# Loading the head of each partition in four strided DMAs instead of one

## The chip, the cores and the metric

The kernel runs on one core of a Trainium2 chip. Such a core has engines that work beside each other and meet only at semaphores: VectorE (DVE) and ScalarE (ACT) copy data inside the on-chip memory, SyncE (SP) issues transfers, and 16 DMA engines move the data between the main memory (HBM) and the on-chip memory, which has 128 partitions. TensorE (PE) and GpSimd (POOL) have no data to work on here. The metric is the device time of one execution in microseconds; three runs of the kernel before gave a median of 197.13 us (197.04 to 197.38).

## The reference

The kernel enlarges images by a factor of two, each pixel becoming a square of four:

```python
batch, channels, h, w = 16, 64, 64, 64          # float32
for i in range(2 * h):
    for j in range(2 * w):
        result[:, :, i, j] = x[:, :, i // 2, j // 2]
```

No arithmetic is done. 16.78 MB are read and 67.11 MB written, 83.89 MB in all.

## The kernel before

The input is taken as 65536 image rows of 64 numbers (256 bytes). Partition p holds 512 rows in a run, so its share of the input is a contiguous 128 KB and its share of the output a contiguous 512 KB (`xp` and `op`, lines 173 to 176). A single tile `mem` holds everything: the whole input of a partition at its far end (`xt`, line 188), and ahead of it room for the enlarged rows.

**Loads.** Lines 192 to 195 issue three loads on SP: rows 0 to 31 of every partition (the head, 8 KB per partition, `HEAD = 32`), rows 32 to 287 (64 KB) and rows 288 to 511 (56 KB). Each covers all 128 partitions, so each is 128 descriptors, 8 for each DMA engine. `begin_before_barrier` (lines 13 to 33) takes the first `EARLY = 3` instructions of SP, which are these loads, and moves them ahead of the barrier at which all engines meet at the start, so that SP issues them before anything else.

**Copies and stores.** The loop of lines 204 to 216 goes over nine groups of rows (`rows`, line 181: 54, 38, 54, 61, ... 62). For each group VectorE copies the first part of the rows enlarged into the room (line 213), ScalarE the rest (line 214), and SP stores the group (line 215). In the first group VectorE has 53 rows and ScalarE one; in the others the shares are about 5 to 3. Groups lie alternately at the start of the room and at its far end, where they overwrite input rows that have been used, so a copy waits for the store two groups before.

**Order of the work.** A framework puts in the semaphores: a copy waits for the loads that brought its rows, a store for the copies of its group. There are eight semaphores for DMAs, used in turn. All transfers are issued by SP and stand in one queue on each DMA engine in the order of issue. `close_early` (lines 80 to 151) arranges the end of the program: all semaphores are cleared early, but for the last store's, on which SP waits at the very end.

Of the kernel before, what the change touches and what calls it, by code (L numbers as in the profile page):

```python
# [6 lines left out]

EARLY = 3  # L10


def begin_before_barrier(nc):
# [5 lines left out]
    sp = mybir.EngineType.SP  # L19
    loads = [i for i in body.instructions if i.engine == sp][:EARLY]  # L20
    for load in loads:
# [132 lines left out]
@with_exitstack  # L154
def kernel(
    ctx: ExitStack,
    tc: tile.TileContext,
    x: bass.AP,
    scale_factor: int,
    out: bass.AP,  # L160
):
    nc = tc.nc
    nc.at_finalize(begin_before_barrier)
    nc.at_finalize(close_early)
    P = nc.NUM_PARTITIONS
    s = int(scale_factor)
    B, C, H, W = x.shape
    R = B * C * H // P
    fdt = x.dtype

    xp = x.rearrange("b c h w -> (b c h) w").rearrange("(p r) w -> p r w", p=P)
    op = out.rearrange("b c (h hd) w -> (b c h) (hd w)", hd=s).rearrange(
        "(p r) w -> p r w", p=P
    )

    rows = [54, 38, 54, 61, 54, 63, 63, 63, 62]
    GROW = s * s
    FREE = 79
    WF = FREE * GROW * W
    assert sum(rows) == R
    mem_pool = ctx.enter_context(tc.tile_pool(name="mem", bufs=1))
    mem = mem_pool.tile([P, WF + R * W], fdt, name="mem")
    xt = mem[:, WF:].rearrange("p (r w) -> p r w", r=R)

    HEAD = 32
    cuts = [0, HEAD, R // 2 + HEAD, R]
    for lo, hi in zip(cuts, cuts[1:]):
        nc.sync.dma_start(out=xt[:, lo:hi], in_=xp[:, lo:hi])  # L195

    def expanded(r0, r1):
        return (
            xt[:, r0:r1].unsqueeze(2).unsqueeze(4).to_broadcast([P, r1 - r0, s, W, s])
        )  # L200

    r0 = 0
    before = (0, 0)
    for n, k in enumerate(rows):
        size = k * GROW * W
        at = 0 if n % 2 == 0 else WF + r0 * W - size
        assert at >= before[1] or at + size <= before[0]
        before = (at, at + size)
        u = mem[:, at : at + size].rearrange(
            "p (k a w b) -> p k a w b", k=k, a=s, w=W  # L210
        )
        kv = k - 1 if n == 0 else k * 5 // 8 & ~1
        nc.vector.tensor_copy(out=u[:, :kv], in_=expanded(r0, r0 + kv))  # L213
        nc.scalar.copy(out=u[:, kv:], in_=expanded(r0 + kv, r0 + k))  # L214
        nc.sync.dma_start(out=op[:, r0 : r0 + k, :], in_=u)  # L215
        r0 += k
# [35 lines left out]
```

## Time and profile before

| what | time or share |
|---|---|
| median of three runs | 197.13 us (197.04 to 197.38) |
| the profiled execution | 196.92 us |
| its span, first to last instruction | 195.6 us |
| VectorE busy | 52.3 us, 27% |
| ScalarE busy | 42.1 us, 21% |
| DMA packets, share of 16 engines' span | 99.2% (1728 packets, 83.89 MB) |
| mean rate over the span | 429 GB/s |
| the three loads, from issue to landing | 4.7, 23.6 and 40.1 us |
| first copy on VectorE, 128x13568 | 14.3 us, from 24.11 us on |

The profile is of one execution on the chip. A row of work names the source line, the engine, the operation and the tiles, with its time; idle time is put down to what ended it. "SPq" is SP's queue of instructions: the transfers that it issues, not their data. The DMA share adds up the packets that the DMA engines moved, as a share of 16 engines' time.

### The profile page before, as it was taken

The page shows a single profiled execution, that of the slowest core. Times are in us where ns is not written, and L with a number is a line of the kernel's source. Part 1 is how long each engine was busy: PE and PEld are TensorE (multiplying, and loading weights), DVE is VectorE, ACT ScalarE, POOL GpSimd, SP SyncE. Part 2 cuts the span into 40 slices and gives each one's busy share as a digit, 9 for nine tenths or more (in the row PEclk, how much of TensorE's full clock was granted, in tenths as well). Part 3 has the DMA queues.
Part 4 walks back from the last instruction along what each step waited for, and adds up shares of the span by engine and source line. Part 5 has one row for each costly group of instructions (what it writes and reads, how often), then busy time and mean ns, then how long its engine had stood idle before and what let it go on. Part 6 is the DMA issues. An engine that isn't in the chain of part 4 may idle for free.

```text
span 195.6 us, 102 instructions
## 1 busy us (share of the span) xinstructions
DVE 52.3 (27%) x9; ACT 42.1 (21%) x10; POOL 0.2 (0%) x4
## 2 busy tenths in 40 slices
DVE  0000099940026091053008204500540073000000
ACT  2000000160029700059500004970000073000000
POOL 0000000000000000000000000000000000000000
DMA  9999989889899989999999899999999999999994
GB/s 429 429 429 429 402 375 563 375 362 543 362 436 390 555 362 418 486 409 409 409 420 532 362 531 433 422 422 422 422 422 422 422 422 422 422 435 545 467 428 208
DMA packets 1728, 83.89 MB, mean 429 GB/s; under 512 B 192, under 2 KB 192, under 8 KB 192
## 3 DMA queue, kind: packets, MB, share of 16 engines
q1 hardware_dynamic: 1728, 83.89, 99.2%
HBM read 16.78 MB, written 67.11 MB: 429 GB/s over the span
## 4 chain that ended last, share of the span: by engine, by line
DMA 65%; ACT 11%; DVE 7%; SPq 0%; issue 0%; DVEq 0%; ACTq 0%
DMA out_dram<-mem 53%; DMA mem<-in_x_dram 12%; ACT mem L214 11%; DVE mem L213 7%; SPq L195 0%; DVEq L213 0%; ACTq L214 0%; SPq L215 0%
## 5 line engine op out<-in xcount | busy, mean ns | idle before, releaser
L213 DVE COPY mem<-mem 128x9728 f32<-128x9728 f32 (+3 forms) x9 | 52.3, 5818 | 110.9 <-DMA out_dram<-mem 86.8
L214 ACT COPY mem<-mem 128x6400 f32<-128x6400 f32 (+5 forms) x9 | 40.8, 4530 | 119.4 <-DMA out_dram<-mem 84.2
L214 ACT ACT_TABLE_LOAD x1 | 1.3, 1283 | 1.7 <-PEq L233 1.7
L233 POOL MEMSET const-bfloat16-1.0<- 128x1 bf16 x1 | 0.1, 102 | 0.0
L233 POOL MEMSET const-uint8-127<- 128x1 uint8 x1 | 0.1, 102 | 0.0
L233 POOL MEMSET const-float32-1.0<- 128x1 f32 x1 | 0.1, 99 | 0.0
L233 POOL MEMSET const-float32-0.0<- 128x1 f32 x1 | 0.1, 98 | 0.2 <-issue 0.2
## 6 DMA issues: line engine op xcount, KB each, us to landing
out_dram<-mem SPq DMA_DIRECT2D x3, 8064.0 KB, 32.4
out_dram<-mem SPq DMA_DIRECT2D x3, 6912.0 KB, 22.9
out_dram<-mem SPq DMA_DIRECT2D x1, 7936.0 KB, 32.3
out_dram<-mem SPq DMA_DIRECT2D x1, 7808.0 KB, 29.3
mem<-in_x_dram SPq DMA_DIRECT2D x1, 7168.0 KB, 40.1
out_dram<-mem SPq DMA_DIRECT2D x1, 4864.0 KB, 26.7
mem<-in_x_dram SPq DMA_DIRECT2D x1, 1024.0 KB, 4.7
mem<-in_x_dram SPq DMA_DIRECT2D x1, 23.6
```

The lines of the kernel that those rows point to most:

```text
L213: nc.vector.tensor_copy(out=u[:, :kv], in_=expanded(r0, r0 + kv))
L214: nc.scalar.copy(out=u[:, kv:], in_=expanded(r0 + kv, r0 + k))
L233: nc = _bacc.Bacc("TRN2", target_bir_lowering=False, num_devices=1)
```

## The change

The head becomes 48 rows (12 KB per partition) instead of 32, and it is loaded by four DMAs instead of one. The first covers partitions 0, 8, 16, ... (16 of them), the second 4, 12, 20, ... (16), the third 2, 6, 10, ... (32) and the fourth all odd ones (64). Each partition's head is still one contiguous piece. The second load then begins at row 48 instead of 32 and still ends at row 287; the third is as before. There are six loads instead of three, and `EARLY` is 6 so that all of them stay ahead of the barrier.

```diff
-EARLY = 3
+EARLY = 6
...
-    HEAD = 32
-    cuts = [0, HEAD, R // 2 + HEAD, R]
+    HEAD = 48
+    for first, step in ((0, 8), (4, 8), (2, 4), (1, 2)):
+        some = slice(first, P, step)
+        nc.sync.dma_start(out=xt[some, :HEAD], in_=xp[some, :HEAD])
+    cuts = [HEAD, R // 2 + 32, R]
     for lo, hi in zip(cuts, cuts[1:]):
         nc.sync.dma_start(out=xt[:, lo:hi], in_=xp[:, lo:hi])
```

## The prediction

> **What bounds the kernel now.** I read the busy table first, then the DMA queue, the chain that ended last, the waits, and short windows over the start. From the page, parts 1, 3 and 4:
>
> ```profile
> span 195.6 us, 102 instructions
> DVE 52.3 (27%) x9; ACT 42.1 (21%) x10; POOL 0.2 (0%) x4
> ...
> q1 hardware_dynamic: 1728, 83.89, 99.2%
> ...
> DMA out_dram<-mem 53%; DMA mem<-in_x_dram 12%; ACT mem L214 11%; DVE mem L213 7%; SPq L195 0%; DVEq L213 0%; ACTq L214 0%; SPq L215 0%
> ```
>
> VectorE and ScalarE work for a quarter of the span; the 16 DMA engines are busy for 99.2% of it. The chain does name copies (11% and 7%), but it is a chain of releases, and those copies run beside transfers queued earlier. The trace's records of single DMA packets settle this: laid end to start they form 16 strings, each of 5.24 MB with no gap over 20 ns, from a first packet at 1.00 to 1.48 us to a last end at 194.78 to 195.21 us; the last write is reported at 195.56 us. So the time is three pieces: about 1.0 us to the first packet, about 194 us of busy engines, 0.35 us to the last report. Only what starts the engines later or earlier, slows a packet, or opens a gap can move it.
>
> The timeline, DMA issues (last column: us to landing) and windows (last two columns: DMA share and GB/s; a packet counts in one window only, so single values swing):
>
> ```profile
> 0.00 1.32 SPq L195 DMA_DIRECT2D mem<-in_x_dram  x3
> 1.72 1.28 ACT L214 ACT_TABLE_LOAD   x1 [1.72 <-PEq L233]
> 24.03 0.41 ACT L214 COPY mem<-mem 128x256 f32<-128x256 f32 x1 [21.03 <-DMA mem<-in_x_dram]
> 24.11 17.29 DVE L213 COPY mem<-mem 128x13568 f32<-128x13568 f32 x2 [24.11 <-DMA mem<-in_x_dram]
> ...
> mem<-in_x_dram SPq DMA_DIRECT2D x1, 1024.0 KB, 4.7
> ...
> 0.00:1.00 1.00, 0.00 (x0) 0.00 (x0) 0.20 (x4) 1.00 0.00 0
> 1.00:1.50 0.50, 0.00 (x0) 0.00 (x0) 0.00 (x0) 1.00 1.26 262
> 1.50:2.00 0.50, 0.00 (x0) 0.28 (x1) 0.00 (x0) 1.00 0.67 213
> 2.00:2.50 0.50, 0.00 (x0) 0.50 (x1) 0.00 (x0) 1.00 1.07 442
> ```
>
> The reader is to see three things. Nothing moves for 1.0 us after the first issue. For another microsecond the rate is about half of the later 429 GB/s. And the first copy starts at 24.11 us, when the second load is in: the 1024 KB head, landed at 4.7 us, is used by nobody alone.
>
> **The change part by part.** The sum is made against the profiled execution: 196.92 us, of which 195.6 are the span, and 0.2 below the median of 197.13.
>
> Bytes and packets: an engine had 8 packets of 8192 B (309 ns when running) and 8 of 65536 B (2418 ns) for the first two loads. It gets 8 of 12288 B and 8 of 61440 B. By the slope between those rows, (2418-309)/57344 = 0.0368 ns per byte, they take 460 and 2267 ns; 8 x (309 + 2418) and 8 x (460 + 2267) ns are 21.8 us both. No change. Three DMAs more are three more 4-byte completion packets per engine, 9 ns each: +0.03.
>
> Issues: three more instructions on SP. The three of before start at 0, 0.42 and 0.89 us, so about 0.45 us each, and SP reaches the barrier at 2.8 instead of 1.4 us. Nobody behind that barrier has work before 24 us except the table load. The queue stays fed: descriptors of the n-th small DMA can start at about 1.0 + 0.45 n us, and one packet of 460 ns per engine covers each step. Were an engine to outrun it, that costs some 0.05 us.
>
> Start: the 16 engines' first packets start between 1003 and 1482 ns (mean 1194), one engine after another while the 128 descriptors are laid out. With 16 descriptors I expect them within about 60 ns. But the engines that began first paid most in their first packets (the head cost 0.1 to 0.65 us more than 8 x 309 ns; mean 0.42), and none ended its first packet before 1558 ns. So the gain is what the two last engines have over the others at the end: 195.21 and 195.15 against about 195.0. I take -0.2; bounds 0 and -0.5 (start spread and a third of the ramp gone).
>
> Rate of the small DMAs: before has no DMA over less than 128 partitions, so the cost is bounded. From below: full rate, 0. From above: each of the eight 12288-byte packets of an engine at twice its duration, 8 x 0.46 = +3.7. The nearest row for "one packet on each of 16 engines, all at once" is the set of first packets, which took 325 to 856 ns, mean 630, twice the 309 of the running ones. I take a doubling for DMA 0 and DMA 1, which are just that (one packet per engine), and steady packets for the other two, which have two and four per engine: 2 x 0.46 = +0.92.
>
> [...]
>
> Waits: the first copy on VectorE waits for five loads instead of two, and the two parts of ScalarE and the first store on SP get the same added waits. All but the last are long done. A wait instruction takes 17 to 50 ns, so VectorE starts up to 0.1 us later behind the landing, and with it the first store (issued at 38.48 us) by up to 0.2 us. What hides this: the engines still work on the third load until 40.04 to 40.61 us, and an issue takes 1.0 to 1.48 us to its first packet, so 39.5 to 39.96. The cover is 0.1 to 0.6 us. If it is gone, the excess, at most 0.1 us, is a gap. I take 0.
>
> The instruction order of the changed kernel puts ScalarE's added waits ahead of its table load. So 1.28 us move from 1.7 us to behind the second load, at 24 us, ahead of the one-row copy of 0.41 us: done by 25.8 us. Only the first store waits for that copy, and VectorE's 14.3 us until 38.4 us cover it by over 12 us; without that cover it would cost 1.3 us. The copies, the nine stores, and the size and order of the third load stay.
>
> Sum: -0.20 + 0.92 + 0.03 = +0.75 us. Span 196.35, that execution 197.7, and on the median's footing 197.9 us.
>
> **The rivals.**
>
> *No DMA is slowed (other side).* The four small DMAs run at full rate and only the start shrinks: -0.17, 196.96 us, at best -0.5, 196.6 us. For it: no packet after the first two of an engine is slow anywhere in the trace, whatever its size, and the second load's packets at its start took 2418 to 2422 ns. Against it: every one of those was part of a 128-partition transfer, in which each engine has its own eight partitions. It decides for faster if the two 16-partition DMAs lose less than the 0.2 us that the start gives. To pass 0.2% (0.39 us, about what a measurement of this kernel can tell from no change) the first packets' excess must shrink too, not only the spread.
>
> *The whole head is slowed.* If neighbouring engines also hinder each other in the 32- and 64-partition DMAs, all eight small packets double: 3.7, less what the start spread lets the engines slip past each other (0.2 to 0.5) and less the 0.2 at the start: about +3.1, 200.2 us. For it: the engines' packets follow in step, 309 ns each, so two that meet once meet again. Against it: these two DMAs together cover 96 partitions, evenly. [...]
>
> *The queue runs dry.* If DMAs 1 to 3 arrive just after the engines are through with the one before, each pays the ramp of 0.42 us again: 3 x 0.42 = +1.26, less 0.2: 198.2 us. For it: 0.45 us per issue against 0.46 us per packet is a tie. Against it: the ramp of the first DMA puts the engines 0.3 us behind the queue.
>
> *The change does not do what it says?* It does start with a smaller DMA, but nobody uses the head earlier: the first copy reads 53 rows and the head has 48, so it still ends its wait with the load of rows 48 to 287. No gain can come from earlier copies.
>
> **How the numbers follow.** Two slowed DMAs 0.33 (own range 197.5 to 198.5); no DMA slowed 0.32, of which 0.10 are faster by over 0.2% and 0.22 within it; whole head 0.27; dry queue 0.08. Slower by over 0.2%: 0.33 + 0.27 + 0.08, less 0.02 for small losses, which go to faster for a ramp that shrinks more than I think: 0.66, within 0.22, faster 0.12. The range goes from 196.7 (leaving out the best starts, about 0.08) to 200.3 (leaving out the upper part of the whole-head case, about 0.1).
>
> **What would show it.** In the profile after: 12288-byte packets of about 460 ns (rival 1) or 900 ns (in DMA 0 and 1 alone, or in all four); first packets within 60 ns of each other; the landing of the load of rows 48 to 287, now 24.0 us, at 24.8 (forecast), 23.8 (rival 1) or 27.1 us (whole head), and the first copy right behind it, with everything later shifted by the same. A gap between the third load and the first store would mean that the added waits matter. I would be wrong if no small packet is slowed, or if the 32- and 64-partition DMAs are slowed too.

## The result and the profile after

The changed kernel takes 199.92 us (median of 4 runs, 199.56 to 200.45) where the kernel before took 197.19 us beside it (197.04 to 197.38): a ratio of 1.014, interval 1.0116 to 1.0165. It is slower by 2.7 us. The forecast was slower, at 197.9 us, in a range of 196.7 to 200.3.

The page of the changed kernel (the profiled execution took 199.96 us), parts 1, 3 and 6; the last column of part 6 is microseconds from issue to landing:

```profile
span 198.6 us, 109 instructions
DVE 52.3 (26%) x9; ACT 42.0 (21%) x10; POOL 0.2 (0%) x4
...
q1 hardware_dynamic: 1776, 83.89, 98.5%
...
mem<-in_x_dram SPq DMA_DIRECT2D x1, 7680.0 KB, 24.5
...
mem<-in_x_dram SPq DMA_DIRECT2D x1, 768.0 KB, 7.0
```

The copies cost what they did. The span is 3.0 us longer, the bytes are the same, and the share of busy DMA engines fell from 99.2 to 98.5%: 0.8% of 195.6 us was 1.6 us not busy, 1.5% of 198.6 us is 3.0, averaged over the 16, so half of the loss is idle engines and the rest slower packets. The largest of the small DMAs, 768 KB over 64 partitions, took 7.0 us to land. At the 429 GB/s of the span before it is 1.8 us of work.

The timeline of the changed kernel over the first 60 us:

```profile
0.00 2.49 SPq L195 DMA_DIRECT2D mem<-in_x_dram  x4
...
2.53 1.06 SPq L198 DMA_DIRECT2D mem<-in_x_dram  x2
27.09 1.28 ACT L217 ACT_TABLE_LOAD   x1 [27.09 <-DMA mem<-in_x_dram]
27.12 17.29 DVE L216 COPY mem<-mem 128x13568 f32<-128x13568 f32 x2 [27.12 <-DMA mem<-in_x_dram]
28.38 0.40 ACT L217 COPY mem<-mem 128x256 f32<-128x256 f32 x1
41.48 3.98 SPq L218 DMA_DIRECT2D out_dram<-mem  x2
```

The first copy starts at 27.12 instead of 24.11 us, right behind the load of rows 48 to 287. All 3.0 us are lost by then, and everything later is shifted by the same: the first store is issued at 41.48 instead of 38.48 us. The table load did move behind that load (1.28 us from 27.09 us on), and VectorE's copy, which ends at 41.41 us, covers it.

The windows of the changed kernel (last two columns: DMA share and GB/s) show where the time goes:

```profile
1.00:1.50 0.50, 0.00 (x0) 0.00 (x0) 0.00 (x0) 1.00 0.85 246
1.50:2.00 0.50, 0.00 (x0) 0.00 (x0) 0.00 (x0) 1.00 0.51 147
...
2.50:3.00 0.50, 0.00 (x0) 0.00 (x0) 0.00 (x0) 1.00 0.97 270
3.00:4.00 1.00, 0.00 (x0) 0.00 (x0) 0.00 (x0) 1.00 0.83 295
4.00:5.00 1.00, 0.00 (x0) 0.00 (x0) 0.00 (x0) 1.00 0.80 283
```

Up to 4 us the engines are mostly busy but move 150 to 350 GB/s; from 4 us on the share falls too. The records of single packets name the pieces. First packets start at 1374 to 1833 ns (before: 1003 to 1482). The first 16 packets take 681 ns on average, the next 16 take 652 and the next 710, where 460 is the running duration. Then 13 engines go on with pauses of 0.15 us at most, and three, done with the 32-partition DMA at 4.0 to 4.2 us, start their first packet of the 64-partition DMA only at 5.82, 5.94 and 6.10 us; it ends at 7.06 to 7.09 us. These three finish the head at about 8.5 us, the others at 5.9 to 6.8, and the load behind lands at 27.00 us, when the last engines are through with it: its last packets end at 26.62 to 26.64 us on three engines and at 24.59 to 25.47 on the other 13. Its first packets are slow too: 2.64 us on average, where 2.27 is the running duration.

For one of the three, linked end to start: first packet 0.37 us later than the earliest of before, four packets in 2.64 instead of 1.84 us (+0.80), the next packet ended 3.07 us later instead of 0.46 (+2.61), +0.05 on the last three. That is 3.83 us over an ideal start at 1.00; the slowest engine of before had lost 0.84 (start 0.48, slow first packet 0.36). The difference, 2.99, is the measured shift of the landing, from 24.01 to 27.00 us.

Three late engines delay the other 13 as well. Those 13 end the third load at 41.49 to 42.38 us, but the first store is issued only at 41.48, when the late copy is done, and its first packets on these engines start at 42.33 to 42.47. Twelve of the 16 engines stand idle there for 0.2 to 1.0 us. In the kernel before, the third load ended at 40.04 to 40.61 us, the store was issued at 38.48, and no engine stood idle.

### The profile page after: what moved, and what is told of

Its sections match the earlier page's. It is cut to its first block, busy times and chain, and to the rows that moved or that the text cites. A ratio compares the mean times of both kernels' runs of the same rounds, so it can differ in the third digit from the quotient of the medians.

```text
span 198.6 us, 109 instructions
## 1 busy us (share of the span) xinstructions
DVE 52.3 (26%) x9; ACT 42.0 (21%) x10; POOL 0.2 (0%) x4
## 3 DMA queue, kind: packets, MB, share of 16 engines
q1 hardware_dynamic: 1776, 83.89, 98.5%
## 4 chain that ended last, share of the span: by engine, by line
DMA 65%; ACT 10%; DVE 7%; SPq 1%; issue 0%; DVEq 0%; ACTq 0%
DMA out_dram<-mem 52%; DMA mem<-in_x_dram 12%; ACT mem L217 10%; DVE mem L216 7%; SPq L195 1%; DVEq L216 0%; SPq L218 0%; ACTq L217 0%
```

## The experiments

Three theories were to be told apart: *sharing* (a DMA over few partitions makes engines hinder each other), *count* (each further DMA ahead of the stream costs), and *length* (pieces of 12288 and 61440 bytes cost). Each kernel was timed beside the kernel before; ratios are to that.

**One head of 48 rows.** The edit against the changed kernel (and `EARLY` 3):

```diff
-    for first, step in ((0, 8), (4, 8), (2, 4), (1, 2)):
-        some = slice(first, P, step)
-        nc.sync.dma_start(out=xt[some, :HEAD], in_=xp[some, :HEAD])
-    cuts = [HEAD, R // 2 + 32, R]
+    cuts = [0, HEAD, R // 2 + 32, R]
```

> The head is 48 rows as in the changed kernel, but in one DMA over all 128 partitions, as before. Sharing theory (packets are slow because a DMA over few partitions makes engines hinder each other) and count theory (each further DMA ahead of the stream costs, whatever its shape): both about 197.2 us, 12288-byte packets at 460 ns after the ramp, issue instructions of 0.37 to 0.43 us. Length theory (pieces of 12288 and 61440 bytes are slow to lay out or to move): issues of 0.59 us for the first two loads, and part of the loss, 197.6 us or more.

Measured: 197.51 us against 197.25, ratio 1.0008 (0.9999 to 1.0017); first two issues of 372 and 424 ns, first packet at 998 ns, 12288-byte packets mostly at 460 ns after the first. The first packets took 0.85 to 1.31 us, longer than the 0.33 to 0.86 us of the 8192-byte ones of before. Length explains 0.3 us at the most; the rest of the loss comes with the split.

**Four DMAs over all partitions.** The head as four times 12 rows (the edit against the run above, and `EARLY` 6):

```diff
-    cuts = [0, HEAD, R // 2 + 32, R]
+    cuts = [0, 12, 24, 36, HEAD, R // 2 + 32, R]
```

> The 48 head rows come in four DMAs of 12 rows, each over all 128 partitions. Sharing theory: nothing is slowed beyond the first ramp, 197.2 us (packets of 3072 bytes at about 121 ns). Count theory: about as slow as the changed kernel, 199.5 to 200 us, with engines that stand idle between the small DMAs and the next load.

Measured: 197.97 us, ratio 1.0039 (1.0026 to 1.0052). Both theories missed: neither nothing nor the whole. Issues are 385 to 432 ns and the first packet starts at 1015 ns, as before. A few engines stood idle around the fourth and fifth DMA, with starts at 4.87, 5.31 and 5.75 us after ends at 4.5 to 4.8. So about a quarter of the loss (0.7 us) comes even where each of the four DMAs covers all partitions, and it has the face of the idle engines above, but shorter.

**Four DMAs over neighbouring partitions.**

```diff
-    for first, step in ((0, 8), (4, 8), (2, 4), (1, 2)):
-        some = slice(first, P, step)
-        nc.sync.dma_start(out=xt[some, :HEAD], in_=xp[some, :HEAD])
+    for lo, hi in ((0, 16), (16, 32), (32, 64), (64, 128)):
+        nc.sync.dma_start(out=xt[lo:hi, :HEAD], in_=xp[lo:hi, :HEAD])
```

> The same four DMA sizes (16, 16, 32 and 64 partitions, 48 rows), but each over neighbouring partitions. Sharing theory: neighbours lie closer together, so the first two DMAs are slowed up to four times instead of twice and the other two about twice: 1.4 + 1.4 + 0.9 + 1.8 us, about 202.5 us, with 12288-byte packets of 0.9 to 1.8 us. Count theory: as the changed kernel, 199.5 to 200 us.

Measured: 201.83 us, ratio 1.022 (1.0203 to 1.0237). The slow packets that sharing foretold are there: an engine's second packet took 1.42 us on average and the third 1.40 (three times the running 0.46; the factor of up to four was an estimate that no run shows), those of the last DMA (64 neighbours) 0.89 to 0.96, twice. The windows of this kernel show the rate held down for as long as these DMAs last:

```profile
2.00:4.00 2.00, 0.00 (x0) 0.61 (x1) 0.00 (x0) 1.00 0.96 129
4.00:6.00 2.00, 0.00 (x0) 0.68 (x1) 0.00 (x0) 1.00 0.88 184
6.00:9.00 3.00, 0.00 (x0) 0.00 (x0) 0.00 (x0) 1.00 1.03 225
```

The engines are busy all that time and move a third to a half. The first packet starts at 1020 ns here, with an issue of 397 ns: the later start of the changed kernel goes with the step between partitions, not with their small number.

**The strided DMAs with 64 KB pieces.**

```diff
-    HEAD = 48
+    HEAD = 256
```

> The four strided DMAs carry 256 rows each partition (64 KB pieces) instead of 48, and rows 256 to 287 follow in a small one over all partitions. This measures the dispute by itself, with packets too long for any start effect. Sharing theory: the packets of the two 16-partition DMAs take about 4.8 us instead of 2.42, and if all four are slowed, eight packets cost 19 us more (216 us); if only the first two, 4.8 us more (about 202 us). Count theory: 65536-byte packets stay at 2.42 us but for the first, and the time is 197.2 to 198 us, because the queue is always ahead.

Measured: 202.39 us, ratio 1.0257 (1.0242 to 1.0272). The windows:

```profile
2.00:12.00 10.00, 0.00 (x0) 0.00 (x0) 0.00 (x0) 1.00 0.81 216
...
14.00:26.00 12.00, 0.00 (x0) 0.00 (x0) 0.00 (x0) 1.00 1.01 437
```

While the two 16-partition DMAs last, the core gets 216 GB/s, half; after them 437. (Windows count a packet where it starts, but the packets say the same: 16 of 65536 bytes in 4.88 us are 215 GB/s.) In packets: the first two of an engine took 4.81 and 4.88 us on average, the third 2.91, and all later ones 2.42, the full rate. So 16 partitions with a step of 8 double a packet, and 32 with a step of 4 or 64 with a step of 2 do not (that the third packet, 2.91 us, is slow on engines that are ahead while others are still in the second DMA is a reading that was not tried).

The doubled packets of the two 16-partition DMAs are shown, then (4.81 and 4.88 us against 2.42); why they take so long no run shows. But in the changed kernel they can account for slow packets before 4 us at most (the run with two DMAs, below, shows for how much of them), and the three idle engines stay unexplained. The next runs are about these.

**Twice the work in each small DMA.**

```diff
-    HEAD = 48
+    HEAD = 96
```

> The changed kernel with 96 head rows instead of 48, so every packet of the four strided DMAs is twice as long (24576 bytes, about 0.91 us at full rate) while the issues stay as far apart. Sharing theory, as the 64 KB run showed it (the packets of the two 16-partition DMAs double, the others do not), and a first packet at 1.4 instead of 1.0 us: 2 x 0.91 + 0.3 to 0.4, about 199.4 us. Dry-queue theory for the three engines that stood idle for 2 us before the 64-partition DMA: with twice the work in the queue none runs dry, so 199.4 us and no idle engine. If that idle time has another cause, it stays: 201 to 201.5 us.

Measured: 199.21 us, ratio 1.0091 (1.0076 to 1.0107), as both expected without idle engines. The engines go on to the 64-partition DMA at 7.0 to 7.9 us without a late one; the second packet took 1.73 us instead of 0.91, nearly the doubling, and the third 1.44. With double the head the kernel is faster than the changed one (a ratio of 1.0091 against 1.014), although the doubled packets cost more.

**The order reversed.**

```diff
-    for first, step in ((0, 8), (4, 8), (2, 4), (1, 2)):
+    for first, step in ((1, 2), (2, 4), (4, 8), (0, 8)):
```

> The same four strided DMAs in the opposite order: 64, 32, 16 and 16 partitions. Sharing costs the same, 0.92 us, and the late first packet 0.3 to 0.4. Dry-queue theory: the first DMA has four packets per engine (1.84 us), so the queue is ahead of the engines from then on, and no engine stands idle: 198.4 us. If the idle engines belong to the 64-partition DMA itself, or to strided DMAs as such, the time stays near 199.9 us.

Measured: 198.51 us, ratio 1.0054 (1.0037 to 1.0071). The DMA issues of this kernel:

```profile
mem<-in_x_dram SPq DMA_DIRECT2D x1, 768.0 KB, 4.5
mem<-in_x_dram SPq DMA_DIRECT2D x1, 384.0 KB, 5.1
mem<-in_x_dram SPq DMA_DIRECT2D x2, 192.0 KB, 5.5
```

The 64-partition DMA lands 4.5 us after its issue instead of 7.0, and no engine stands idle before 5.3 us. The same four DMAs, the same bytes: the order alone is worth 1.7 us of the 2.7 (a loss of 1.0 us remains, each loss taken against the kernel before beside it). The idle engines do not belong to the 64-partition DMA as such but to what stands ahead of it. The doubled packets show here, behind a running stream: an engine's last two packets of the head took 0.53 and 0.77 us on average, and the first of the next load 2.72 instead of 2.27.

**Three strided DMAs, none of 16 partitions** (`EARLY` 5).

```diff
-    for first, step in ((0, 8), (4, 8), (2, 4), (1, 2)):
+    for first, step in ((0, 4), (2, 4), (1, 2)):
```

> Three strided DMAs instead of four, over 32, 32 and 64 partitions (0, 4, 8, ...; 2, 6, 10, ...; all odd ones), 48 rows. Sharing theory with the finding that 32 evenly strided partitions are not slowed: no doubling; each DMA has two packets per engine or more, so the queue stays ahead; what is left is the later first packet, 0.3 to 0.4 us: 197.6 us. If the partial DMAs cost in another way (idle engines, slow packets), 198.5 us or more.

Measured: 199.26 us, ratio 1.0093 (1.0070 to 1.0116). Sharing with a fed queue said 197.6, and it missed. The DMA issues and one window of this kernel:

```profile
mem<-in_x_dram SPq DMA_DIRECT2D x2, 384.0 KB, 3.7
mem<-in_x_dram SPq DMA_DIRECT2D x1, 768.0 KB, 7.5
```

```profile
2.00:3.00 1.00, 0.00 (x0) 0.00 (x0) 0.00 (x0) 1.00 0.91 356
...
4.00:5.00 1.00, 0.00 (x0) 0.00 (x0) 0.00 (x0) 1.00 0.89 111
```

No steady doubling: after the first of each engine, nearly all packets of the two 32-partition DMAs are at 460 to 505 ns. But at the change to the 64-partition DMA 14 of 16 engines stop: its first packet takes 1.1 to 2.2 us, and the packets that start in the microsecond from 4 us on make only 111 GB/s. The DMA had been issued at 1.23 us; the first packets of the stopped engines end at 5.1 to 7.1 us. The stall needs no 16-partition DMA and no doubled packet.

**The changed kernel again.**

> The changed kernel once more, for a second profile. If the idle time of three engines before the 64-partition DMA is part of the change, it shows again: packets of that DMA that start 1.5 to 2 us after the others, and a landing of the load of rows 48 to 287 near 27 us. If it was an accident of the one profiled execution, all engines go on at about 4.2 us, and the span is about 196.8 us.

Measured: 199.43 us, span 198.1. One engine was late instead of three: its first packet of the 64-partition DMA ended at 5.97 us, and that DMA landed 6.2 us after its issue. So the effect was there in both profiled executions, and its size differed between them.

**Two DMAs of 64 partitions** (`EARLY` 4).

```diff
-    for first, step in ((0, 8), (4, 8), (2, 4), (1, 2)):
+    for first, step in ((0, 2), (1, 2)):
```

> The 48 head rows in two strided DMAs of 64 partitions (even ones, then odd ones). [...] Late-descriptor theory (in the run with three strided DMAs most engines' first packet of the 64-partition DMA took 1.3 to 2.2 us instead of 0.46 although the queue was issued 1.9 us earlier; descriptors of a DMA that follows strided ones arrive late): first packets of the second DMA are long again, at 3.7 us and later, 198.5 us or more. If the stall comes at a time (4 to 6 us after the first issue) and not at a change of DMA, packets in the middle of the second DMA are slow.

Measured: 197.85 us, ratio 1.0016 (1.0005 to 1.0026). Windows of this kernel:

```profile
3.00:4.00 1.00, 0.00 (x0) 0.00 (x0) 0.00 (x0) 1.00 1.04 442
4.00:5.00 1.00, 0.00 (x0) 0.00 (x0) 0.00 (x0) 1.00 1.10 467
```

Full rate across the change of DMA, which starts at 3.8 us, no doubled packet, no late engine. What is left is the start: issue 550 ns, first packet at 1334. The first packets took 1.02 us on average although nothing is doubled here. An engine's fourth packet ended at 4.00 us on average; in the changed kernel, whose engines started at the same time (1.53 us on average, 1.52 here), it ended at 4.18. So up to 4 us the two small DMAs cost the changed kernel about 0.2 us more than this one; the rest of its slow packets is a slow start that a DMA over 64 partitions has as well. The second DMA had been issued 3.2 us before it was needed, the load behind it for 4.4. So strided DMAs as such do not stall, and the time of 4 to 6 us after the start does not either.

**The large loads held back.** One load of rows 47 to 511, which overlaps the head by a row and so waits for all four small DMAs (`EARLY` 4):

```diff
-    cuts = [HEAD, R // 2 + 32, R]
+    cuts = [HEAD - 1, R]
```

> The four strided DMAs as in the changed kernel, but the rest of the input comes in one load (rows 47 to 511) that is issued only after the four have landed; the total time is not comparable (copies begin later), only the first microseconds are read. If descriptors of the large loads, laid out behind the small ones, are what makes some engines late for the 64-partition DMA, no engine is late now: all its packets start by 4.5 us and it lands by 6.9 us. If the strided DMAs alone do it, one to three engines still start that DMA 0.4 to 2 us late and it lands at 8 us or later.

Measured: no late engine; the 64-partition DMA lands on 14 engines by 6.7 us and on two at 7.1, as the 32-partition DMA before it had landed on two engines 0.4 us after the rest. Its windows, where the changed kernel had 283 GB/s from 4 to 5 us and 393 from 5 to 6:

```profile
4.00:5.00 1.00, 0.00 (x0) 0.00 (x0) 0.00 (x0) 1.00 0.98 406
5.00:6.00 1.00, 0.00 (x0) 0.00 (x0) 0.00 (x0) 1.00 0.91 381
```

The second window holds only the end of the head here, so the first is the one to compare. It speaks for the large loads as the cause, but it is one execution of something that varies between executions.

**No head at all**, against the kernel before (`EARLY` 2):

```diff
-    cuts = [0, HEAD, R // 2 + HEAD, R]
+    cuts = [0, R // 2 + HEAD, R]
```

> The kernel before without a head: rows 0 to 287 in one load, rows 288 to 511 in the second. Since the first copy waits for row 53, and so for the second load, in both kernels, nobody misses the head: if the head has a use it is a shorter start ramp (first packets of 8 KB instead of 36 KB), worth 0.2 us at most; 197.2 to 197.5 us.

Measured: 197.46 us against 197.45, ratio 1.0003 (0.9993 to 1.0012). The old head had no measurable use: no copy starts on it.

**The large loads 1.1 us later** (`EARLY` 4):

```diff
+    nc.sync.dma_start(out=xt[0:1, 0:1], in_=xp[0:1, 0:1])
     cuts = [HEAD, R // 2 + 32, R]
```

> The changed kernel, but the two large loads are issued about 1.5 us later: a DMA of one row of partition 0 (it rewrites the same data) waits for the first strided DMA to land, at about 3.3 us, and stands in front of them on SP. They come at about 4.0 us instead of 2.5, and their packets are needed from 5.9 us on, so the queue should not run dry for them. Large-load theory (laying out the 128-partition loads right behind the 64-partition DMA is what makes single engines late for that DMA): no late engine, 0.9 us of doubled packets and 0.35 us of late start are left, with 0.1 for the added row: 198.4 to 198.7 us. If late engines come from the strided DMAs alone, or from the small DMAs following each other too closely, the time stays at 199.5 us or more.

Measured: 199.60 us, ratio 1.0114 (1.0086 to 1.0143), as bad as the changed kernel. The timeline and the DMA issues:

```profile
3.26 0.32 SPq L196 DMA_DIRECT2D mem<-in_x_dram  x1
3.63 0.83 SPq L199 DMA_DIRECT2D mem<-in_x_dram  x2
```

```profile
mem<-in_x_dram SPq DMA_DIRECT2D x1, 768.0 KB, 7.1
```

The large loads were issued at 3.63 and 4.04 us, over 1.7 us behind the 64-partition DMA (1.91 us). Three engines were late for it all the same: first packets from 4.96 to 5.24 us that take 1.6 to 1.8 us. And the large load, needed from 6.2 us on, was late too: several engines waited until 7.0 to 7.8 us, or had first packets of 3.4 to 3.8 us instead of 2.27. The theory that a large load right behind is the cause falls in that form. That its laying out disturbs whoever needs descriptors just then (4 to 6 us here) is not excluded.

What stays open is why these engines wait, and why only some do. That the descriptors of the DMA come late is a reading: the trace has no record of descriptors, only of idle engines and long first packets. What the runs show is when: the DMA was issued while the engines were already moving data, and only 2.1 to 3.3 us before they needed it. This lead does not settle it alone. In the run with three strided DMAs the engines reached the second one, over 32 partitions, 2.1 to 2.7 us after its issue, and but for one pause of 0.2 us none stopped; they reached the 64-partition DMA behind it 2.5 to 3.0 us after its issue, and 14 of 16 stopped.

## Why the prediction was right or wrong

*Direction and range* were right, the point was not: +2.7 us where +0.75 was forecast. That the range held the result is luck: the two slowed DMAs had a range of their own up to 198.5 us, and only the whole-head rival, which did not happen, carried it to 200.3.

*No gain from earlier copies* was right. The first copy waits for the load of rows 48 to 287, and the kernel before takes the same time without any head.

*Added waits and the moved table load* at nothing were right: the first copy starts 0.12 us after the last landing, and the first store is issued 0.08 us after the copy (before: 0.10 and 0.09). The gap between the third load and the first store, named as the sign of costly waits, is there, but it comes from the late landing.

*The start, -0.2*, had the wrong sign. I took the spread of 479 ns over the engines for the laying out of 128 descriptors. With 16 descriptors it is 459 ns, so the number of descriptors is not what sets it. And I took 0.45 us for an issue; a strided one takes 0.57 to 0.59, the first 592 instead of 372, and the first packet comes 0.37 us later. All strided runs have it (first packet at 1334 to 1402 ns), none of the runs without a step has it (998 to 1078 ns).

*The doubling of the two 16-partition DMAs, +0.92*, is there: 4.85 instead of 2.42 us with long packets, 32 and 64 strided partitions unslowed. What causes it no run shows. And the term was too large for this place in the queue. By the fourth packet the changed kernel is 0.2 us behind the one with two DMAs of 64 partitions, where nothing is doubled: there the first packet of an engine is slow anyway, 1.02 us on average, where the changed kernel's took 0.68. Placed last, behind a running stream, the same two DMAs showed 0.4 us in their own packets and 0.45 in the first of the next load, about the 0.92. The saying that no packet of the kernel before is slow after the first two of an engine had small exceptions: one took 469 ns and one 349 instead of 309.

*A fed queue, 0.05 us*, is the step that failed most, and it holds the larger part of what is missing. I set the arrival of descriptors at 1.0 us plus 0.45 per issue, from the first DMA, which found all engines idle. On the late engines the data of the 64-partition DMA, by this estimate, began to flow 4.7 us after its issue (1.90 to about 6.6 us, the end of its first packet less its 0.46), in the second profile 3.6 us, with three DMAs 3.4 to 5.4 us. So the dry-queue rival, at 0.08, named the larger part of the loss, priced at 0.42 us per restart where a restart cost 2.6 us on the engines that it hit. The 1.0 us held for the first DMA of before (issued until 0.37, first packet at 1.00 us), not for the 64-partition DMAs above, which were issued into busy engines.

*The whole-head rival* came nearest in time (200.2 us) for a wrong reason: the packets of the 64-partition DMA are at 460 ns in the median, and at 2.42 us with long pieces, so it is not slowed as it said.

## What to carry to other kernels

Where the DMA engines were busy for 99.2% of the span and nothing started on the first load, finer first loads gained nothing here; even the old head was worth nothing measurable (a ratio of 1.0003 without it). If a transfer must be split by partitions, evenly strided halves cost least here (0.4 us against 2.7; that this comes from the four packets which each DMA had for each engine was not shown); and the largest DMA first was better than last (a loss of 1.0 us against 2.7). A later DMA issued 3.2 us or more ahead of its need was on time in the runs with two DMAs and with the order reversed; others, at 2.1 to 3.3 us, often were not. That is no safe limit, as these leads overlap. A loss at a change of DMA on a few engines was a loss for the whole kernel, since the landing came with the last engine: three late ones put off the first copy by 3.0 us, and with it the first store on all.

## What the hardware did that was not expected

A first issue with a step between partitions took 0.55 to 0.62 us on SP, one without 0.37 to 0.44; the plain load behind strided ones took 0.58 to 0.61 us as well, and behind the four DMAs over neighbours 0.58. Partition sets with a step of 2 or 4 ran at full rate here (step 2: 442 to 467 GB/s in the windows of the two-DMA run; both: packets of 2.42 us in the run with 64 KB pieces), 16 partitions with a step of 8 at half (216 GB/s), and 16 neighbours at about a third (packets of 1.4 us instead of 0.46). Some engines that reached a DMA within 2 to 3 us of its issue waited 1 to 2 us for it: one engine in the second profile of the changed kernel, three in the first, nearly all with three strided DMAs.
